# Gate columns in matmuls of 512 tokens, heads transposed before they are split, and the pairs of branch C ahead of those of branch B, in a three-branch encoder layer

## The chip, the cores and the metric

The kernel runs on one core of one Trainium2 chip. Its time is the device time of one execution in microseconds (us); runs are compared by their median. Inside the core, TensorE (PE) multiplies matrices, VectorE (DVE) and ScalarE (ACT) read PE's results out of PSUM and work on them, GpSimd (POOL) does further element-wise work on SBUF, and SyncE (SP) issues every DMA. Each engine takes its instructions strictly in the order that was fixed when the program was built; engines wait for one another by semaphores.

## The reference

One layer over 2048 tokens of width 1024, all in float32. `h` is the LayerNorm of `x`, and one projection of `h` (7592 columns) feeds three branches and all gates:

```
h = layer_norm(x)
proj = h @ w_in        # a_q a_k a_v a_gate  i_q i_k i_w  b_q b_k b_v b_gate  c_q c_gate  m_gate
A: scores = sum_h i_w * relu(i_q . i_k);  the 256 best keys of each query;  8-head attention on these
B: 4 heads, softmax(q0 k0) - lam * softmax(q1 k1), times v, RMS norm
C: 4-head cross attention of c_q into 256 memory tokens (mem @ w_mem_kv)
y_r = (o_r * silu(gate_r)) @ w_proj_r          for r = A, B, C
merged = sum_r sigmoid(m_gate_r) * y_r
out = layer_norm(alpha * h + merged @ w_out)
```

Queries and keys of A, B and of the index scores are rotated (RoPE) on a part of their channels. Keys are limited to the query's own chunk of 64 tokens and all before it.

## The kernel before, in words

**Precision.** Every float32 product is made of three matmuls (`mm3`, L71 to L74): each operand is split into a high part H, rounded to PE's fast float32 format (fp32r), and a rest L = value - H. `split` (L62 to L69) makes the two: a copy into H on one engine, a subtraction into L on another.

**Stages in the order of the text.** The activations are kept transposed, channels on partitions, in four tiles `hP` of 256 tokens each (1024 tokens, a half), and each half is projected in turn.

1. `dense_ai(0)`: queries of A, the index projections, for half 0; `topk_group` finds the 256 best keys of each query for blocks of 128 tokens by a search over the 32 bits of the score (counts on DVE and ACT); `dense_b(0)`, then the same for half 1, two more `topk_group`s, `dense_b(1)`.
2. Attention B: 4 heads x 16 blocks = 64 blocks. Logits (`lg`, L623, L624), row minimum on DVE, exponentials on ACT, a combination on DVE, transposes (`pt`, L703), a split of these by ACT and DVE, and the product with v (`ops`, L709).
3. Attention A: 16 blocks x 4 units of two heads: `lg`, DVE (`AP`, L626), ACT, transposes (`apt`, L777), split (`apr`), product (`aops`, L782).
4. `dense_g(1)`, reload of half 0, `dense_g(0)`: c_q, the SiLU gates (`sg`) and the merge gates (`tm`), 20 jobs of 256 columns for each half (PSUM tile `dps`), with the memory's keys and values between.
5. For each pair of blocks (256 tokens): branch B, then branch C (`attn_c`, cross attention, PSUM tile `cps`), each followed by its output projection (`branch`, PSUM tile `yps`), and a sum on POOL that is stored as `mg_d`.
6. Branch A's projection (`stage1`), then for each pair the output projection (`stage2`, PSUM tile `fz`) and the last LayerNorm.

**What sets the order.** A scheduler places every engine's instructions by a planned timeline. Text order is only a priority: where an attention would leave PE idle, later work whose inputs and buffers are there is put in between. So the gate jobs of step 4 stand between the matmuls of steps 1 and 2, and steps 5 and 6 between those of step 3. Work put between in this way is called filler here.

**What the change touches.** `heads_out` (L212) writes queries and keys transposed to DRAM. Each of its two blocks of 128 tokens is split by DVE first (`dt`: a CAST at L68 and a TENSOR_TENSOR at L69), H and L of a head side by side; PE then transposes the fp32r tile (L223) and ACT copies the result into `de` (L225). RoPE (L133 to L136) runs on POOL ahead of it. `dense` (L244) computes a gate job: for c_q, the merge gates and C's SiLU gate the weights `w` are the stationary operand, for the SiLU gates of A and B the tokens are. Either way a matmul has 256 moving columns. `emit` (L297) evaluates and stores; `gated` (L827) multiplies an attention output by its gate, transposes it and splits it; `yw` is the pool of the tiles `yt` (8 of them, YT) in which merge gates are loaded and branch outputs are made.

Of the kernel before, what the change touches and what calls it, by code (L numbers as in the profile page):

```python
# [23 lines left out]
NP = NB // 2  # L24
KT = D // 128
# [13 lines left out]
YT = 8  # L39
# [14 lines left out]
def tile_layer(ctx, tc, x, mem, ln_in_g, ln_in_b, w_in, w_mem_kv, diff_lambda, diff_norm_g,  # L54
# [28 lines left out]
    qa_d = [[dram(f"qa_d{j}_{p}", [4, 128, 256]) for p in range(NP)] for j in range(2)]  # L83
    qi_d = [[dram(f"qi_d{j}_{p}", [128, 4, 256]) for p in range(NP)] for j in range(2)]
# [5 lines left out]
    qb_d = [[dram(f"qb_d{j}_{p}", [4, 128, 256]) for p in range(NP)] for j in range(2)]  # L90
    kb_d = [[dram(f"kb_d{j}_{p}", [4, 128, 256]) for p in range(NP)] for j in range(2)]
# [3 lines left out]
    cq_d = [dram(f"cq_d{p}", [128, 4, 2, 256]) for p in range(NP)]  # L95
    sg_d = [[dram(f"sg_d{r}_{p}", [128, 4, 256] if r == 2 else [2, 128, 512]) for p in range(NP)] for r in range(3)]
    tm_d = [[dram(f"tm_d{r}_{p}", [128, KT, 256]) for p in range(NP)] for r in range(3)]
    oa_d = [dram(f"oa_d{b}", [128, 512]) for b in range(NB)]
    ob_d = [dram(f"ob_d{b}", [128, 512]) for b in range(NB)]
    mg_d = [dram(f"mg_d{p}", [128, KT, 256]) for p in range(NP)]  # L100

# [45 lines left out]
    hT, hP = {}, {}  # L147
    early = [True]
    last_rope = [None]

    def hT_tile(b):
        if b % 2 == 0:
            hP[b // 2] = hTp.tile([128, 2, KT, 256], F32R, name=f"hP{b // 2}", tag=f"hP{b // 2 % 4}")
        hT[b] = hP[b // 2][:, :, :, 128 * (b % 2):128 * (b % 2 + 1)]
        return hT[b]
# [31 lines left out]
    def prologue(b, banks):  # L187
# [11 lines left out]
        to_hT(hT_tile(b), xt, banks)  # L199

    def save_hT(b):
        xt = p1.tile([128, KT, 128], F32, name="xt")
        G.tensor_tensor(xt, hT[b][:, 0].bitcast(F32), hT[b][:, 1].bitcast(F32), op=ALU.add)
        SP.dma_start(ht_d[b], xt)

    def reload(b):
        xt = p1.tile([128, KT, 128], F32, name="xt")
        SP.dma_start(xt, ht_d[b])
        h = hT_tile(b)
        split(h[:, 0], h[:, 1], xt, A, V)  # L210

    def heads_out(o, nh, d, dup, stores, p):  # L212
        e = dp.tile([128, nh, 2, 128], F32R, name="de")
        for i in range(2):
            t = dp.tile([128, nh, 2 * dup, d], F32R, name="dt" if nh > 1 else "dt1", bufs=3 if nh > 1 else 2)
            src = o[:, i, :, None, :].to_broadcast([128, nh, dup, d]) if dup > 1 else o[:, i, :, None, :]
            split(t[:, :, 0:dup], t[:, :, dup:2 * dup], src, V, V)
            if i:
                pt = dq2.tile([128, nh, 128], F32R, name="psT")
            else:  # L220
                pt = dqs.tile([128, nh, 128], F32R, name="dpt", bufs=1)
# [4 lines left out]
        for dst, c0, c1 in stores:  # L226
            SP.dma_start(dst, e.bitcast(F32)[:, c0:c1].rearrange("p c i t -> p c (i t)"))
# [16 lines left out]
    def dense(kind, half, cols, idx, w=None):  # L244
        n = sum(c for _, c in cols)
        if w is None:
            w = load_win(cols, A if early[0] else G)
        for p in range(4 * half, 4 * half + 4):
            ps = dqs.tile([128, 2, 256], F32, name="dps")
            for i in range(2):  # L250
                if kind in ("cq", "tm") or (kind == "sg" and idx[0] == 2):
                    c = slice(i * 128, (i + 1) * 128)
                    h = hP[p]
                    for k in range(KT):
                        mm3(ps[:, i], w[:, 0, k, c], w[:, 1, k, c], h[:, 0, k], h[:, 1, k], k == 0, k == KT - 1)
                    continue
                h = hT[2 * p + i]
# [5 lines left out]
    def dense_ai01(half):  # L263
# [16 lines left out]
        for p in range(4 * half, 4 * half + 4):  # L280
            ps = [dqs.tile([128, 512], F32, name="dps") for _ in range(2)]
            for a in range(2):
                for i in range(2):
                    h = hT[2 * p + i]
# [11 lines left out]

    def emit(kind, idx, p, ps, n, o=None):  # L297
        if kind == "cq":
            for i in range(2):
                o = dw.tile([128, 2, 256], F32R, name="do", bufs=3)  # L300
                with tc.high_priority():
                    split(o[:, 0], o[:, 1], ps[:, i], A, V)
                SP.dma_start(cq_d[p][:, 2 * idx + i], o.bitcast(F32))
            return
        if kind != "bv" and o is None:
            o = dw.tile([128, 2, 256], F32, name="do", bufs=3)
        if kind in ("sg", "tm"):
            r, j = idx
            with tc.high_priority():
                A.activation(o, ps, AF.Tanh, scale=0.5)  # L310
                if kind == "sg":
                    V.scalar_tensor_tensor(o, o, 1.0, ps, op0=ALU.add, op1=ALU.mult)
            if kind == "tm" or r == 2:
                SP.dma_start((sg_d if kind == "sg" else tm_d)[r][p][:, 2 * j:2 * j + 2], o)
            else:
                SP.dma_start(sg_d[r][p][:, :, j * 256:(j + 1) * 256].rearrange("i p c -> p i c"), o)
            return
        if kind == "bv":
            v = dp.tile([128, 2, 2, 2, 128], F32R, name="de")
# [27 lines left out]
        else:  # L347
# [8 lines left out]
            for i in range(2):  # L356
                PE.transpose(pt[:, i], t[:, i].rearrange("p a d -> p (a d)"), idr)
# [713 lines left out]
```

## Time and profile before

| | |
|---|---|
| median of 3 runs | 2966.72 us (2961.39 to 2970.45) |
| the profiled execution: its span, first to last instruction | 2965.9 us |
| PE busy | 2830.5 us, 95% |
| DVE busy | 2279.2 us, 77% |
| ACT / POOL busy | 1442.6 us, 49% / 983.2 us, 33% |
| DMA engines busy, mean | about 41% |

No time of its own is recorded for the profiled execution beside its span; the span lies 0.8 us under the median of the runs. A busy share counts from an instruction's start to its end. Successive matmuls overlap, so the step from one matmul's start to the next start, not the duration, is what one costs in a stream.

### The profile page before, as it was taken

How to read it: one execution, taken by the hardware profiler on the slowest of the kernel's cores; microseconds unless marked ns; L12 is line 12 of the kernel's file. 1: busy time of each engine (PE TensorE's matmuls, PEld its weight loads, DVE VectorE, ACT ScalarE, POOL GpSimd, SP SyncE). 2: the span in 40 equal slices, each digit the busy share in tenths (PEclk: the TensorE clock that was granted, in tenths of full speed). 3: DMA queues.
4: the chain of work that ended last, by engine and by line, in shares of the span. 5: the costliest groups of instructions: out<-in, count | busy, mean ns of one | idle time of the engine just before them, and what ended most of it. 6: DMA issues, size and time to landing. Idle time of an engine off the chain costs nothing. (4 is left out here: it accounts for less than half of the span.)

```text
span 2965.9 us, 57460 instructions
## 1 busy us (share of the span) xinstructions
PE 2830.5 (95%) x21616; PEld 2715.7 (92%) x21616; DVE 2279.2 (77%) x5309; ACT 1442.6 (49%) x2806; POOL 983.2 (33%) x1064
## 2 busy tenths in 40 slices
PE   7979998999999998999999999999999999988998
PEld 6979998999999998999999999988999999978887
DVE  6499988999899998676667766658787777776655
ACT  4345673677266772333344334446566556544100
POOL 6663547242522236323324222302222222200221
PEclk9999999999999999999999999999999999999999
DMA  6554434433232234624234242273433333256532
GB/s 208 171 191 138 159 113 156 133 119 114 94 101 76 82 93 147 201 73 140 89 118 142 77 128 80 75 242 110 133 114 119 102 113 102 86 172 224 172 131 79
DMA packets 320949, 379.47 MB, mean 128 GB/s; under 512 B 26400, under 2 KB 236832, under 8 KB 320160
## 3 DMA queue, kind: packets, MB, share of 16 engines
q1 hardware_dynamic: 320672, 375.80, 40.2%
q8 instruction: 171, 2.80, 0.4%
q14 instruction: 106, 0.87, 0.1%
HBM read 236.02 MB, written 139.69 MB: 127 GB/s over the span
## 5 line engine op out<-in xcount | busy, mean ns | idle before, releaser
L72 PE MATMUL dps<-hP,w 128*128 128x256 f32 x2048 | 582.6, 284 | 15.1 <-DVE do L69 9.9
L74 PE MATMUL dps<-hP,w 128*128 128x256 f32 x2048 | 581.7, 284 | 0.0
L73 PE MATMUL dps<-hP,w 128*128 128x256 f32 x2048 | 581.2, 284 | 0.0
L72 PE MATMUL dps<-w,hP 128*128 128x256 f32 (+1 forms) x1664 | 491.1, 296 | 12.5 <-POOL w L64 3.1
L73 PE MATMUL dps<-w,hP 128*128 128x256 f32 (+1 forms) x1664 | 490.0, 295 | 0.0
L74 PE MATMUL dps<-w,hP 128*128 128x256 f32 (+1 forms) x1664 | 487.9, 294 | 0.0
L72 PEld LDWEIGHTS dps<-hP,w 128*128 128x128 f32 x2048 | 392.6, 192 | 21.6 <-DVE do L69 10.7
L74 PEld LDWEIGHTS dps<-hP,w 128*128 128x128 f32 x2048 | 392.5, 192 | 4.4 <-POOL w L69 0.3
L73 PEld LDWEIGHTS dps<-hP,w 128*128 128x128 f32 x2048 | 392.7, 192 | 3.6
L533 ACT ACTIVATE ja<-sall,thr 128x1280 bf16<-128x1280 f32 (+4 forms) x224 | 302.2, 1349 | 122.6 <-DVE thr L529 107.1
L64 POOL TENSOR_SCALAR w<-wr 128x1024 fp32r<-128x1024 f32 x120 | 135.5, 1129 | 629.5 <-PE dps L74 404.9
L72 PEld LDWEIGHTS dps<-w,hP 128*128 128x128 f32 x1664 | 324.0, 195 | 16.8 <-issue 4.3
L69 POOL TENSOR_TENSOR w<-wr,w 128x1024 fp32r<-128x1024 f32 (+1 forms) x128 | 332.1, 2595 | 15.0 <-ACT w L66 6.9
L520 DVE TENSOR_SCALAR_CACHE_REDUCE jd<-sall,thr 128x1408 bf16<-128x1408 f32 (+6 forms) x231 | 330.9, 1433 | 5.9
L73 PEld LDWEIGHTS dps<-w,hP 128*128 128x128 f32 x1664 | 324.3, 195 | 1.8
L74 PEld LDWEIGHTS dps<-w,hP 128*128 128x128 f32 x1664 | 323.8, 195 | 2.2
L691 ACT ACTIVATE P<-P,nm 128x128 f32<-128x128 f32 (+15 forms) x128 | 154.1, 1204 | 197.8 <-DVE nm L690 187.5
L626 DVE CUSTOM_DVE_ANT_0 AP<-lg,bias 128x512 f32<-128x512 f32 (+3 forms) x304 | 181.9, 619 | 68.4 <-PE lg L624 25.1
L66 ACT CAST apr<-apt 128x512 fp32r<-128x512 f32 (+1 forms) x288 | 158.4, 563 | 141.7 <-PE apt L777 108.4
L633 DVE TENSOR_SCALAR_CACHE_REDUCE P<-lg 128x512 f32<-128x512 f32 (+3 forms) x288 | 170.4, 596 | 72.3 <-PE lg L624 71.2
L493 DVE SCALAR_TENSOR_TENSOR sall<-ir,iw,sall 128x512 f32<-128x512 f32 (+3 forms) x266 | 217.1, 865 | 8.9 <-ACT ir L489 8.0
L782 PE MATMUL aops<-apr,VA 128*128 128x256 f32 x1088 | 206.7, 297 | 16.8 <-DVE apr L69 6.7
(249 smaller groups left out, 7109.2 us busy)
## 6 DMA issues: line engine op xcount, KB each, us to landing
wr<-in_w_in_dram SPq DMA_DIRECT2D x112, 512.0 KB, 3.9
tm_d<-do SPq DMA_DIRECT2D x96, 256.0 KB, 2.1
bq<-qb_d SPq DMA_DIRECT2D x128, 128.0 KB, 3.1
aq<-qa_d SPq DMA_DIRECT2D x128, 128.0 KB, 3.1
yt<-tm_d SPq DMA_DIRECT2D x64, 256.0 KB, 3.6
sg_d<-do SPq DMA_DIRECT2D x48, 256.0 KB, 2.1
ys<-sg_d SPq DMA_DIRECT2D x48, 256.0 KB, 3.1
facc<-mg_d SPq DMA_DIRECT2D x48, 256.0 KB, 4.1
```

The lines of the kernel that those rows point to most:

```text
L66: A.copy(H, src)
L69: el.tensor_tensor(L, src, H.bitcast(F32), op=ALU.subtract)
L72: PE.matmul(ps, lH, rH, start=start, stop=False)
L73: PE.matmul(ps, lH, rL, start=False, stop=False)
L74: PE.matmul(ps, lL, rH, start=False, stop=stop)
L493: V.scalar_tensor_tensor(s[:, c0:c0 + cn], r[:, :cn], iw[:, h:h + 1], s[:, c0:c0 + cn], op0=ALU.mult, op1=ALU.add)
L520: V.tensor_scalar(jd[:, :L], sc[b], t.bitcast(F32)[:, i:i + 1], None, op0=op, op1=ALU.add, accum_out=dst[:, i:i + 1])
L533: A.activation(ja[:, :L], sc[b], AF.Sign, bias=thr.bitcast(F32)[:, i:i + 1], scale=-1.0, accum_out=cnt[:, i:i + 1])
L626: V.tensor_tensor_reduce(P[:, c0:c0 + cn], ps[:, :cn], bias[:, c0:c0 + cn], scale=-0.125, scalar=-LOW, op0=ALU.add, op1=ALU.min, accum_out ...
L633: V.tensor_scalar(P[:, c0:c0 + n0], ps[:, :n0], -0.125, None, op0=ALU.mult, op1=ALU.min, accum_out=mx[:, col, nch:nch + 1])
L691: A.activation(p[:, :L], p[:, :L], AF.Exp, bias=nm[:, c:c + 1], scale=-1.0, accum_out=sm[:, c:c + 1])
L782: PE.matmul(o_ps.rearrange("p a d -> p (a d)"), VA[:, k0 + i], pr[:, a, i].rearrange("p e q -> p (e q)"), start=(k0 + i == 0 and a == 0), ...
```

## The change

- **Gates by 512 tokens.** The four `hP` tiles become one tile `H4` (two groups of 512 tokens). Every gate job now has the weights stationary and 512 tokens moving: a matmul of 512 columns in place of two of 256. The jobs, their weights and the number of PSUM tiles stay; all gates are stored transposed.
- **Heads in 32 bits.** `heads_out` transposes the float32 projection itself, two groups of up to 128 channels at a time, and splits the transposed result straight out of PSUM (ACT copies H, DVE subtracts). The CAST and the subtraction ahead of the transposes go. Layouts in DRAM and the loads of queries and keys follow; index queries are loaded by four DMAs of 32 partitions where one of 128 was.
- **`gated`**: transposes the ungated output, multiplies on DVE, copies on ACT, subtracts on POOL.
- **All eight pairs of branch C, then all of branch B.** C's results are stored as `mc_d` and loaded again for the sum with B's.
- **YT is 4** in place of 8.

```diff
-YT = 8
+YT = 4
+    H4 = hTp.tile([128, 2, 2, KT, 512], F32R, name="H4")
+    def hT_of(b):
+        return H4[:, b // 4 % 2, :, :, 128 * (b % 4):128 * (b % 4 + 1)]
-    def heads_out(o, nh, d, dup, stores, p):
-        e = dp.tile([128, nh, 2, 128], F32R, name="de")
-        for i in range(2):
-            t = dp.tile([128, nh, 2 * dup, d], F32R, name="dt" if nh > 1 else "dt1", bufs=3 if nh > 1 else 2)
-            src = o[:, i, :, None, :].to_broadcast([128, nh, dup, d]) if dup > 1 else o[:, i, :, None, :]
-            split(t[:, :, 0:dup], t[:, :, dup:2 * dup], src, V, V)
-            if i:
-                pt = dq2.tile([128, nh, 128], F32R, name="psT")
-            else:
-                pt = dqs.tile([128, nh, 128], F32R, name="dpt", bufs=1)
-            for c in range(nh):
-                PE.transpose(pt[:, c], t[:, c].rearrange("p a d -> p (a d)"), idr)
-            with tc.high_priority():
-                A.copy(e[:, :, i], pt)
+    def heads_out(o, groups, stores):
+        n = len(groups)
+        e = dp.tile([128, 2, n, 2, 128], F32R, name="de", bufs=4)
+        turn[0] ^= 1
+        if turn[0]:
+            pt = dq2.tile([128, n, 2, 128], F32, name="psT")
+        else:
+            pt = dqs.tile([128, n, 2, 128], F32, name="dpt", bufs=1)
+        for u, (c0, cn) in enumerate(groups):
+            for i in range(2):
+                PE.transpose(pt[:cn, u, i], o[:, i, c0:c0 + cn], idf)
+        for u0, u1 in ((0, 2),) if groups[-1][1] == 128 else ((0, n - 1), (n - 1, n)):
+            cn = groups[u0][1]
             with tc.high_priority():
+                split(e[:cn, 0, u0:u1], e[:cn, 1, u0:u1], pt[:cn, u0:u1], A, V)
 ...
     def dense(kind, half, cols, idx, w=None):
+        if kind in ("cq", "sg", "tm"):
+            for q in range(2 * half, 2 * half + 2):
+                for g in range(2):
+                    c = slice(g * 128, (g + 1) * 128)
+                    ps = dqs.tile([128, 512], F32, name="dps")
+                    for k in range(KT):
+                        mm3(ps, w[:, 0, k, c], w[:, 1, k, c], H4[:, q % 2, 0, k], H4[:, q % 2, 1, k], k == 0, k == KT - 1)
+                    with tc.high_priority():
+                        emit_gate(kind, idx, g, q, ps)
+            return
 ...
+    def emit_gate(kind, idx, g, q, ps):
 ...
+        r, j = idx
+        o = dw.tile([128, 512], F32, name="do", bufs=3)
+        A.activation(o, ps, AF.Tanh, scale=0.5)
+        if kind == "sg":
+            V.scalar_tensor_tensor(o, o, 1.0, ps, op0=ALU.add, op1=ALU.mult)
+        SP.dma_start((sg_d if kind == "sg" else tm_d)[r][q][:, 2 * j + g], o)
 ...
-                SP.dma_start(qi.bitcast(F32), qi_d[j][b // 2][:, :, (b % 2) * 128:(b % 2 + 1) * 128])
+                for r in range(4):
+                    SP.dma_start(qi.bitcast(F32)[32 * r:32 * r + 32], src[r // 2])
 ...
-        eng.tensor_tensor(o, o, s, op=ALU.mult)
 ...
-            A.activation(oT[:, 0, :, t], ps, AF.Copy, scale=0.5)
-            V.scalar_tensor_tensor(oT[:, 1, :, t], ps, 0.5, oT[:, 0, :, t].bitcast(F32), op0=ALU.mult, op1=ALU.subtract)
+            V.scalar_tensor_tensor(s, ps, 0.5, s, op0=ALU.mult, op1=ALU.mult)
+            A.copy(oT[:, 0, :, t], s)
+            G.tensor_tensor(oT[:, 1, :, t], s, oT[:, 0, :, t].bitcast(F32), op=ALU.subtract)
 ...
-    for p in range(NP):
-        T = []
-        for r, w, mix in ((1, wb, gated_b), (2, wc, gated_c)):
+    for r, w, mix in ((2, wc, gated_c), (1, wb, gated_b)):
+        for p in range(NP):
 ...
                 branch(yq, w, oT, u, t, 1)
-        for u in range(4):
-            G.tensor_tensor(T[u], T[u], T[4 + u], op=ALU.add)
-            SP.dma_start(mg_d[p][:, 2 * u:2 * u + 2], T[u])
+                if r == 2:
+                    SP.dma_start(mc_d[p][:, 2 * u:2 * u + 2], t)
+                    continue
+                c = yw.tile([128, 2, 256], F32, name="yt")
+                SP.dma_start(c, mc_d[p][:, 2 * u:2 * u + 2])
+                G.tensor_tensor(t, t, c, op=ALU.add)
+                SP.dma_start(mg_d[p][:, 2 * u:2 * u + 2], t)
```

Where the change stands in the programs is shown by the order of the engines' rows (line, operation, tiles as out<-in, shape, how many in a run). First PE in the first half of attention B (`lg`, `ops` and `pt` are the attention's, `dps` is gate filler). Before:

```order
L709 MATMUL ops<-vg,pr 128x256 x7
L703 MATMUL pt<-idf,P 128x128 x5
L623 MATMUL lg<-kg,bq 128x512
L624 MATMUL lg<-kg,bq 128x512
L623 MATMUL lg<-kg,bq 128x512
L624 MATMUL lg<-kg,bq 128x512
L74 MATMUL dps<-hP_25611,w 128x256
```

and now, at the same place:

```order
L715 MATMUL ops<-vg,pr 128x256 x15
L709 MATMUL pt<-idf,P 128x128 x6
L629 MATMUL lg<-kg,bq 128x512
L630 MATMUL lg<-kg,bq 128x512
L629 MATMUL lg<-kg,bq 128x512
L630 MATMUL lg<-kg,bq 128x512
L75 MATMUL dps<-H_269,w 128x512
```

In the gap behind the second pair of logits, up to the next `lg`, 22 gate matmuls of 256 columns stand before and 20 of 512 now: about as many instructions, and nearly twice the columns.

Second, PE in the last third of attention B (`yps` is branch C's projection, `cps` its cross attention). Before:

```order
L709 MATMUL ops<-vg,pr 128x256 x7
L703 MATMUL pt<-idf,P 128x128 x6
L623 MATMUL lg<-kg,bq 128x512
L624 MATMUL lg<-kg,bq 128x512
L623 MATMUL lg<-kg,bq 128x512
L624 MATMUL lg<-kg,bq 128x512
L73 MATMUL dps<-hP_25620,w 128x256
```

and now:

```order
L74 MATMUL cps<-mkT,cqT 128x256
L715 MATMUL ops<-vg,pr 128x256 x15
L709 MATMUL pt<-idf,P 128x128 x8
L629 MATMUL lg<-kg,bq 128x384
L630 MATMUL lg<-kg,bq 128x384
L629 MATMUL lg<-kg,bq 128x512
L630 MATMUL lg<-kg,bq 128x512
L73 MATMUL yps<-yoT,H_269 128x256
```

The gates are over by then: branch C's work is the filler, which before began only with attention A.

Third, PE at the end of attention A, ahead of the first `fz` (`gT` is a transpose of branch A's output). Before:

```order
L72 MATMUL yps<-yoT,whP_33902 128x256
L73 MATMUL yps<-yoT,whP_33902 128x256
L74 MATMUL yps<-yoT,whP_33902 128x256
L833 MATMUL gT<-idf,fo 128x128 x8
L72 MATMUL fz<-whP_34237,fmT 128x512
```

and now:

```order
L788 MATMUL aops<-apr,VA_14503 128x256 x3
L783 MATMUL apt<-idf,AP 128x128 x4
L788 MATMUL aops<-apr,VA_14503 128x256 x8
L794 MATMUL ot<-idf,os 128x128 x4
L73 MATMUL fz<-H_269,fmT 128x512
```

Nothing stands any more between the last instruction of attention A and the first output projection.

## Rows read from the trace of the kernel before

**Rows 1.** The page: span; busy time of each engine (share of the span).
```profile
span 2965.9 us, 57460 instructions
PE 2830.5 (95%) x21616; PEld 2715.7 (92%) x21616; DVE 2279.2 (77%) x5309; ACT 1442.6 (49%) x2806; POOL 983.2 (33%) x1064
```
**Rows 2.** Busy time by stretch: from:to, length, each engine's busy time, clock, DMA.
```profile
0.00:1200.60 1200.60, 1112.45 (x8886) 1097.35 (x8887) 1051.03 (x1804) 674.17 (x1183) 554.38 (x533) 0.97 0.41 133
1200.60:1637.00 436.40, 433.10 (x3381) 419.13 (x3380) 310.41 (x1060) 172.59 (x341) 146.20 (x208) 1.00 0.39 119
1637.00:1963.50 326.50, 325.10 (x2551) 316.04 (x2550) 202.87 (x668) 125.85 (x226) 87.12 (x132) 1.00 0.33 103
1963.50:2739.80 776.30, 741.47 (x5685) 698.55 (x5683) 586.04 (x1593) 449.18 (x1025) 145.74 (x144) 0.99 0.45 134
2739.80:2966.00 226.20, 218.40 (x1120) 184.61 (x1120) 128.89 (x188) 20.86 (x35) 49.76 (x47) 0.98 0.38 132
```
**Rows 3.** Timeline of PE, gate matmuls of 256 columns: start, duration.
```profile
749.73 0.28 PE L74 MATMUL dps<-hP,w 128*128 128x256 f32 x1
...
755.97 0.28 PE L72 MATMUL dps<-hP,w 128*128 128x256 f32 x1
```
**Rows 4.** Timeline of PE, output projection, matmuls of 512 columns.
```profile
2849.68 0.39 PE L72 MATMUL fz<-whP,fmT 128*128 128x512 f32 x1
...
2855.98 0.39 PE L72 MATMUL fz<-whP,fmT 128*128 128x512 f32 x1
```
**Rows 5.** Timeline of PE: transposes of fp32r tiles, then of a float32 tile.
```profile
648.79 0.46 PE L223 MATMUL dpt<-idr,dt 128*128 128x128 f32 x4
649.09 0.51 PE L223 MATMUL psT<-idr,dt 128*128 128x128 f32 x4
649.44 0.35 PE L74 MATMUL dps<-hP,w 128*128 128x256 f32 x1
...
2301.80 0.60 PE L777 MATMUL apt<-idf,AP 128*128 128x128 f32 x4
2302.15 0.37 PE L73 MATMUL yps<-yoT,whP 128*128 128x256 f32 x1
```
**Rows 6.** Line 223, PE's idle time before it (us, times).
```profile
  DVE dt L69: 38.4, 28
```
**Rows 7.** Groups of DVE instructions: busy us, mean ns, idle before.
```profile
L69 DVE TENSOR_TENSOR dt<-do,dt 128x256 fp32r<-128x256 f32 x128 | 76.1, 620 | 0.2
L68 DVE CAST dt<-do 128x256 fp32r<-128x256 f32 x128 | 50.0, 415 | 42.8 <-POOL do L136 31.9 <-PE dpt L223 8.7 <-PE psT L223 1.4
```
**Rows 8.** The same for branch C's cross attention, in attention A's stretch.
```profile
L870 DVE TENSOR_REDUCE cmx<-cps 128x2 f32<-128x512 f32 x32 | 22.0, 686 | 2.3 <-PE cps L74 2.3
L69 DVE TENSOR_TENSOR cpr<-cps,cpr 128x512 fp32r<-128x512 f32 x32 | 21.9, 684 | 1.4 <-ACT cpr L66 1.1
L899 DVE TENSOR_TENSOR yoT<-co,yoT 128x256 fp32r<-128x256 f32 x32 | 14.4, 451 | 0.6 <-ACT yoT L898 0.4
L896 DVE TENSOR_TENSOR co<-co,cps 128x256 f32<-128x256 f32 x32 | 13.2, 414 | 0.8 <-ACT co L895 0.4
```
**Rows 9.** Timeline of DVE in attention A.
```profile
2302.94 0.69 DVE L626 CUSTOM_DVE_ANT_0 AP<-lg,bias 128x512 f32<-128x512 f32 x1
2303.55 0.68 DVE L845 SCALAR_TENSOR_TENSOR yt<-yt,yps 128x512 f32<-128x512 f32 x1
```
**Rows 10.** Busy time of the first third of attention A.
```profile
1963.50:2218.00 254.50, 241.11 (x1829) 224.97 (x1828) 203.89 (x632) 163.93 (x410) 51.77 (x52) 0.99 0.50 145
```
**Rows 11.** The chain that ended last, from attention A to `fz`.
```profile
2732.79 6.21 DMA facc<-mg_d
2739.78 0.80 PE fz L72
```
**Rows 12.** POOL's sum of `yt`; loads of `yt` (KB, us to landing).
```profile
L922 POOL TENSOR_TENSOR yt<-yt 128x512 f32<-128x512 f32 x32 | 43.1, 1347 | 117.3 <-DVE yt L845 103.1 <-DVE crc L877 14.2
yt<-tm_d SPq DMA_DIRECT2D x64, 256.0 KB, 3.6
```

More of the change, by code (lines that the diff above doesn't have):

```diff
@@ L24 @@
 NP = NB // 2
+NQ = NB // 4
 KT = D // 128
@@ L82, in tile_layer @@
     h_d = [dram(f"h_d{b}", [128, D]) for b in range(NB)]
-    qa_d = [[dram(f"qa_d{j}_{p}", [4, 128, 256]) for p in range(NP)] for j in range(2)]
-    qi_d = [[dram(f"qi_d{j}_{p}", [128, 4, 256]) for p in range(NP)] for j in range(2)]
+    qa_d = [[dram(f"qa_d{j}_{p}", [2, 256, 256]) for p in range(NP)] for j in range(2)]
+    qi_d = [[dram(f"qi_d{j}_{p}", [2, 128, 256]) for p in range(NP)] for j in range(2)]
     ka_d = dram("ka_d", [128, S])
@@ L89, in tile_layer @@
     bias_d = [dram(f"bias_d{b}", [128, (b + 1) * 128], BF16) for b in range(NB)]
-    qb_d = [[dram(f"qb_d{j}_{p}", [4, 128, 256]) for p in range(NP)] for j in range(2)]
-    kb_d = [[dram(f"kb_d{j}_{p}", [4, 128, 256]) for p in range(NP)] for j in range(2)]
+    qb_d = [[dram(f"qb_d{j}_{p}", [2, 256, 256]) for p in range(NP)] for j in range(2)]
+    kb_d = [[dram(f"kb_d{j}_{q}", [2, 256, 512]) for q in range(NQ)] for j in range(2)]
     vb_d = [[dram(f"vb_d{j}_{p}", [2, 128, 2, 256]) for p in range(NP)] for j in range(2)]
@@ L250, in dense @@
             for i in range(2):
[L251 to L257, printed above, removed]
+                h = hT_of(2 * p + i)
                 for k in range(KT):
@@ L283, in dense_ai01 @@
                 for i in range(2):
-                    h = hT[2 * p + i]
+                    h = hT_of(2 * p + i)
                     for k in range(4):
@@ L295, in dense_ai01 @@
                 emit("ai1", None, p, None, W_AI - 256, o[1])
-    def emit(kind, idx, p, ps, n, o=None):
-        if kind == "cq":
-            for i in range(2):
-                o = dw.tile([128, 2, 256], F32R, name="do", bufs=3)
-                with tc.high_priority():
-                    split(o[:, 0], o[:, 1], ps[:, i], A, V)
-                SP.dma_start(cq_d[p][:, 2 * idx + i], o.bitcast(F32))
-            return
+    def emit_gate(kind, idx, g, q, ps):
+        if kind == "cq":
+            for a in range(2):
+                o = dw.tile([128, 512], F32R, name="do", bufs=3)
+                if a == 0:
+                    A.copy(o, ps)
+                    H = o
+                else:
+                    V.tensor_tensor(o, ps, H.bitcast(F32), op=ALU.subtract)
+                SP.dma_start(cq_d[q][:, 2 * idx + g, a], o.bitcast(F32))
+            return
+        r, j = idx
[4 more added lines that the diff above has]
+        SP.dma_start((sg_d if kind == "sg" else tm_d)[r][q][:, 2 * j + g], o)
+    def emit(kind, idx, p, ps, n, o=None):
         if kind != "bv" and o is None:
             o = dw.tile([128, 2, 256], F32, name="do", bufs=3)
[L307 to L317, printed above, removed]
         if kind == "bv":
-            v = dp.tile([128, 2, 2, 2, 128], F32R, name="de")
+            v = dp.tile([128, 2, 2, 2, 128], F32R, name="de", bufs=4)
             with tc.high_priority():
@@ L904, in gated_b @@
             SP.dma_start(o, ob_d[b])
-            gated(yp, yq, "cps", o, yp.tile([128, 512], F32, name="ys"), 1, b, G, oT)
+            gated(yp, yq, "cps", o, yp.tile([128, 4, 128], F32, name="ys"), 1, b, oT)
     def gated_c(p, oT):
```

99 lines of the change are left out of this document (47 added, 52 removed).

## The prediction

> **What bounds the kernel now.** I read the page first, then the busy time by stretch, then the timeline of PE for the step between matmuls, and last who waited for whom. The page shows PE busy for 95% of the 2965.9 us span and DVE for 77% [rows 1]. That share counts overlapping durations, so I took the step between starts instead: 52 gate matmuls of 256 columns from 749.73 to 755.97 are 0.120 us each [rows 3], 27 of 512 columns from 2849.68 to 2855.98 are 0.233 [rows 4]. I cut the span where the work changes: before the first transpose of attention B (1200.6 us), B's first 40 blocks (436.4), its last 24 (326.5), attention A up to the first output projection (776.3), and the rest (226.2) [rows 2]. The reader should see that PE is busy 93 to 100% of every stretch while DVE comes close only in the first (1051 of 1201) and falls to 203 of 326.5 and 129 of 226 behind it. So PE's queue sets the time, and two things matter: how much PE has to do, and in which order, because a stretch with too little filler waits for DVE instead. The granted clock is 0.97 to 1.00 of its upper level, 2.4 GHz, in all five [rows 2], so little is to be had there.
>
> The span lies 0.8 us under the median of the runs, so I make the sum against 2965.9 and read it as the median.
>
> **The change part by part.**
>
> *Gates.* 20 jobs, two halves, 192 matmuls of 256 columns each half-job: 7680 x 0.120 = 921.6 us. Now 3840 x 0.2333 = 896.0. That is 25.6 us less, if a gate matmul of 512 columns runs at the step of the output projection, which has the same shape and the same kind of operands. The bounds are 25.6 less and nothing (a step of two old ones, 0.240): the same columns pass, so I see no cause for a loss. The number of PSUM tiles to empty stays (each now 24 matmuls, 5.6 us, before 48, 5.8 us), so ACT, DVE and POOL get no more to do per gate. The projection rows show 0.233 at 512 columns. The Trainium skill, in "TensorE: Matmul & The Clock Gate", section "Back-to-back issue gap", gives about 131 ns as the sustained step at 512 columns, and about 216 for an isolated one. By 131 the gates alone would fall by some 419 us; the trace does not agree, neither with that nor with 216 (it has 233), and the measured step decides.
>
> *Heads.* 544 transposes of fp32r tiles become 256 of float32 tiles. Eight of the old take 0.65 us from 648.79 to 649.44, 0.081 each; four float32 ones take 0.35, 0.0875 each [rows 5]. 544 x 0.081 - 256 x 0.0875 = 44.2 - 22.4 = 21.8 us less on PE. On DVE a CAST (0.415) and a subtraction (0.620) [rows 7] per 128 tokens leave the path in front of the transposes; one subtraction out of PSUM per 256 tokens comes in behind them. PE stood idle 38.4 us in 28 waits for exactly that DVE work [rows 6]. What is late next is RoPE on POOL, for which DVE itself waited 31.9 us [rows 7]; PE now waits for it directly. Each wait gets shorter by the two DVE steps, 1.035 us: 28 x 1.035 = 29 us, between 0 (POOL late anyway) and 38.4. I take 29.
>
> *Order.* This is the part that costs. The gaps of the attention were filled by the planner with about as many gate matmuls as before, 22 of 256 columns against 20 of 512 in the gap shown. Counted over the whole program, the stretches become:
>
> - Before B: 7262 matmuls of 256 columns, now 3072 of 256 and 2286 of 512: 901.9 against 871.4 us, 30.5 more; transposes 21.8 less, 16 memory transposes moved here, 1.4 more; waits 29 less. 1200.6 + 10.1 - 29 = 1182.
> - B's first 40 blocks: 2059 of 256 (247.1 us) become 1524 of 512 and 192 of 256 (378.6), minus the memory's 1.4 us: 130 more. PE was busy 433 of 436 there [rows 2], so all of it lies on the path: 566.
> - B's last 24 blocks: 1581 gate matmuls (189.7 us) go, 30 of 512 stay (7.0). Branch C comes in: 136 matmuls of `cps` (16.3), 52 narrow ones (3), 56 transposes (4.9), 288 of `yps` (34.6). PE has 123 us less to do: 204. Now DVE is late: 202.9 us were its own [rows 2]; C's four groups are 71.5 us for 320 `cps` matmuls [rows 8], 136 of them 30.4; 13 more weight splits and 12 `yt` at 0.69 [rows 9] are 17. That is 250 us. Lower end: successive instructions start 0.61 apart and not 0.69 [rows 9], 250 x 0.88 = 220. Upper end: in the first third of A DVE reached 204 of 254.5, 80% [rows 10], 250 / 0.80 = 312. I take 262, near the middle. Queued behind a late DVE are the splits of `pt`, and behind them PE's `ops`.
> - A to the first `fz`: 330 matmuls of 256 (39.6), 136 `cps` (16.3), 52 narrow ones (3), 44 transposes (3.9) and 2 logits (0.5) have moved forward, 63 us. 5 of them were cover: before, 40 `yps` stood beside the wait from 2732.79 to 2739.78 for the load of `mg_d` [rows 11]; now nothing does. 776.3 - 63 + 5 = 718.
> - The rest: 12 transposes less, 225.
>
> Sum: 1182 + 566 + 262 + 718 + 225 = 2953 us, 13 less than 2965.9. In one line: 47 us of PE work and 29 of waits are saved, 58 are given back where PE waits for DVE, 5 at the seam.
>
> *What I cost at nothing.* `gated`: the product moves from POOL or DVE ahead of the transposes to DVE behind them, and a subtraction from DVE to POOL. 32 of each, on engines that PE does not wait for; without that cover 32 x 0.7 us. C's results take a way through DRAM: 64 transfers more, and 92 more for other layouts. YT 4: a step of B holds two tiles for a load of 3.6 us [rows 12], 24 matmuls (2.9), DVE (0.7), POOL's sum (1.35) [rows 12] and a store of about the load's length, 12 us, two steps at a time, so one step every 6 us. The 32 steps stand in a stretch of some 300 us, 9 us apart. That cover gone, SP would hold back loads of A queued behind a `yt`.
>
> **The rivals.**
>
> *PE stays full.* If DVE's load in the last third of B hides behind PE, the stretch takes its PE work, 204, and the seam its old length: 2953 - 58 - 5 = 2890. For it: DVE's rows overlap, and ACT shares the splits. Against it: even at 0.61 a step DVE needs 220.
>
> *The tail of B starves, slower.* The place is the same, B's last 24 blocks, and the price is the upper end: 312 instead of 262 gives 3003. For it: where PE had too little filler before, at the start of A, both engines together left a fifth of DVE's time unused [rows 10]. Against it: there the chain through ACT was that of A, with 4 tiles `AP` for 1024-wide exponentials; B's blocks overlap better (PE lost 1.4 us of 326.5 [rows 2]). It turns to slower than before from 275 us in that stretch.
>
> *Nothing saved by the width.* If a gate step of 512 is 0.240 or the planner's gaps swallow the waits of the heads again, 26 or 29 us return: 2980.
>
> *The step of the skill's page.* With 0.131 the time would be near 2535.
>
> **How the numbers follow.** The forecast's own case, 2930 to 2975, has 0.50; PE full 0.19; the starved tail 0.21; nothing saved 0.09; the page's step 0.01. About 0.3% (9 us) is what a measurement of this kernel tells from no change: faster is below 2958, slower above 2976. Of the forecast's own case 0.31 lies below 2958 and 0.17 between. Faster: 0.31 + 0.19 + 0.01 and a little of the others, 0.52. Same: 0.18. Slower: 0.30. The range takes in PE full at the low end, 2890, and the starved tail with part of the heads' 29 us lost, 3018.
>
> **What would show it.** Gate matmuls of 512 columns 0.233 apart; no wait for a `dt`, and waits of the heads' transposes for POOL's L136 in their place, under 15 us. First transpose of B at about 1182, its 41st block at 1748, A's first transpose at 2010, `fz` at 2728. In B's last 24 blocks DVE over 90% busy and PE under 85%. The forecast is wrong if PE is busy over 95% there (then the time is under 2920), if the stretch before B still takes 1200 us, or if SP's waits on `yt` show up in front of A's loads.

## The result and the profile after

The changed kernel takes 3031.8 us (median of 4 runs, 3031.3 to 3032.7), the kernel before 2967.0 beside it: ratio 1.0217, 95% interval 1.0202 to 1.0232. It is slower by 65 us; the forecast was 2953 and its range ended at 3018.

The page of the changed kernel, answering to [rows 1]: busy time of each engine, with its share of the span.

```profile
span 3029.5 us, 49112 instructions
PE 2823.2 (93%) x17488; PEld 2509.3 (83%) x17488; DVE 2196.4 (72%) x5053; ACT 1400.0 (46%) x2718; POOL 1014.4 (33%) x1080
```

Every engine but POOL is less busy than before, and the span is 64 us longer. So work was saved, and more than that went into waits. Its busy time by stretch, cut at the same five places as [rows 2]:

```profile
0.00:1216.50 1216.50, 1117.36 (x6712) 1006.32 (x6712) 999.04 (x1573) 638.01 (x1105) 570.25 (x539) 0.97 0.41 132
1216.50:1780.80 564.30, 558.74 (x3020) 480.43 (x3019) 312.99 (x1057) 188.32 (x365) 191.40 (x238) 1.00 0.38 114
1780.80:2050.70 269.90, 232.80 (x1536) 201.99 (x1534) 228.04 (x782) 141.18 (x298) 72.36 (x137) 0.96 0.42 124
2050.70:2805.00 754.30, 697.33 (x5120) 637.29 (x5119) 531.04 (x1463) 412.79 (x918) 127.92 (x117) 0.98 0.45 138
2805.00:3029.50 224.50, 216.92 (x1108) 183.33 (x1108) 125.24 (x181) 19.68 (x33) 52.45 (x49) 0.98 0.37 127
```

| stretch | before | forecast | measured | miss |
|---|---|---|---|---|
| before B | 1200.6 | 1182 | 1216.5 | +34.5 |
| B, first 40 blocks | 436.4 | 566 | 564.3 | -1.7 |
| B, last 24 blocks | 326.5 | 262 | 269.9 | +7.9 |
| A to the first `fz` | 776.3 | 718 | 754.3 | +36.3 |
| the rest | 226.1 | 225 | 224.5 | -0.5 |

The three stretches in the middle and at the end came out as worked out, with PE at 86% in B's last 24 blocks (233 of 270; 100% before) and DVE at 84%, a little short of the 90% that I had named. Two failed: the one in front of B, over the 1200 us that the forecast named as a sign of being wrong, and A's. Three views follow.

First, the gates' step. Of a run of gate matmuls in the timeline of PE (start, duration), the first and the last of 13:

```profile
699.69 0.39 PE L74 MATMUL dps<-H,w 128*128 128x512 f32 x1
...
702.41 0.39 PE L74 MATMUL dps<-H,w 128*128 128x512 f32 x1
```

2.72 us for 12 steps: 0.227, better than the 0.233 taken from [rows 4]. 3840 of them are 870 us, 51 under the 921.6 that the forecast counted for the old ones, and 44 under them at the step of 0.119 used in the counts below. The width does save PE's time.

Second, the heads. What PE waited for at line 223's transposes (us in total, times, longest), before and now:

```profile
PE psT L223 <- DVE dt L69: 13.3, 8, 6.1
PE dpt L223 <- DVE dt L69: 12.3, 8, 3.8
```
```profile
PE psT L223 <- POOL do L138: 10.6, 6, 4.2
PE dpt L223 <- POOL do L138: 0.2, 1, 0.2
```

The 38.4 us in 28 waits of [rows 6] are not PE's alone: the row adds the idle time of the weight loads (PEld), which have a row of their own and run beside the matmuls. On PE it was 25.6 us in 16 waits. The waits for `dt` are gone, and 10.8 us of waits for RoPE on POOL have come in their place: 14.8 saved where 29 were credited.

Third, the indexer ahead of B. It scores block after block for top-k: `ips` on PE, relu to `ir` on ACT, a weighted sum to `sall` on DVE. Its blocks 13 and 14 begin at 835.1, 862.2 and end at 889.0 in the kernel before, 27 us each; in the changed one at 807.7, 850.7 and 892.9, 43 and 42. Groups by line of that stretch, 808 to 893 us, of the changed kernel (busy us, mean ns, idle before); a third of the gate matmuls is in the row of each of lines 73 to 75:

```profile
L73 PE MATMUL dps<-H,w 128*128 128x512 f32 x104 | 40.6, 391 | 0.0
L490 PE MATMUL ips<-KI,qi 128*128 128x256 f32 x122 | 17.9, 277 | 0.0
L499 DVE SCALAR_TENSOR_TENSOR sall<-ir,iw,sall 128x512 f32<-128x512 f32 (+2 forms) x56 | 48.1, 920 | 29.7 <-ACT ir L495 29.7
```

The same stretch, 793 to 846.5 us, of e4 (heads alone, gates of 256; below):

```profile
L73 PE MATMUL dps<-H,w 128*128 128x256 f32 x110 | 31.2, 284 | 0.0
L505 PE MATMUL ips<-KI,qi 128*128 128x256 f32 x120 | 22.6, 277 | 0.0
L514 DVE SCALAR_TENSOR_TENSOR sall<-ir,iw,sall 128x512 f32<-128x512 f32 (+3 forms) x56 | 43.5, 831 | 3.6 <-ACT ir L510 3.2
```

Between about 120 `ips` in both stand 312 gate matmuls where there were 330: nearly as many, each nearly twice as long. DVE, which is busy 90 of the 96 us from 750 to 846 in e4, now stands idle 29.7 us for scores, and the search behind it starts later. The last scan of top-k on DVE, of before, e4, the changed kernel and e12 (the width alone):

```profile
1171.97 4.42 DVE L568 TENSOR_TENSOR_SCAN pf<-ones,ja 128x2048 f16<-128x2048 bf16 x1
```
```profile
1122.94 5.26 DVE L589 TENSOR_TENSOR_SCAN pf<-ones,ja 128x2048 f16<-128x2048 bf16 x1
```
```profile
1186.80 5.71 DVE L574 TENSOR_TENSOR_SCAN pf<-ones,ja 128x2048 f16<-128x2048 bf16 x1
```
```profile
1237.22 6.61 DVE L573 TENSOR_TENSOR_SCAN pf<-ones,ja 128x2048 f16<-128x2048 bf16 x1 [2.83 <-POOL ja L570]
```

The heads alone bring the last scan of top-k forward by 49 us; with the width behind them it comes 55 later again (e2, 1177.83), in the whole change 64.

What of PE's work counts in front of B shows when the stretch is cut at the last `ips`, behind which no score waits for PE any more. The row of the last run of them, before, e4, e2 (heads and width) and changed:

```profile
915.08 0.40 PE L484 MATMUL ips<-KI,qi 128*128 128x256 f32 x2
873.25 0.40 PE L505 MATMUL ips<-KI,qi 128*128 128x256 f32 x2
921.73 0.64 PE L490 MATMUL ips<-KI,qi 128*128 128x256 f32 x4
930.73 0.64 PE L490 MATMUL ips<-KI,qi 128*128 128x256 f32 x4
```

| kernel | last `ips` starts | PE work up to it | difference | from there to B | PE work in that |
|---|---|---|---|---|---|
| before | 915 | 796 | 119 | 285 | 262 |
| e4 | 873 | 746 | 127 | 288 | 263 |
| e2 | 922 | 801 | 121 | 286 | 256 |
| changed | 931 | 801 | 130 | 285 | 256 |
| e12 | 975 | 845 | 130 | 292 | 260 |
| e10 | 927 | 801 | 126 | 263 | 172 |
| e11 | 875 | 746 | 129 | 282 | 248 |

PE work is counted as in the next section. Up to the last score the time is PE's work and 119 to 131 us of waits, in all sixteen kernels that were measured. Behind it 282 to 292 us pass in fifteen of them, and 263 in e10. With the width PE has 55 us more to do in front of the last score (e4 to e2): 1168 gates of 512 columns, 265 us, stand there in place of 1765 of 256, 210 us. Behind the last score B waits for top-k: SP issues the store of the last mask (`pf`) and after it the first load of `kg`, with which B begins. Before, changed, e10:

```profile
1183.78 0.32 SPq L572 DMA_DIRECT2D bias_d<-pf  x1
1188.86 0.59 SPq L651 DMA_DIRECT2D kg<-kb_d  x1
```
```profile
1197.86 0.32 SPq L578 DMA_DIRECT2D bias_d<-pf  x1
1201.50 0.61 SPq L657 DMA_DIRECT2D kg<-kb_d  x1
```
```profile
1162.85 14.69 SPq L589 DMA_DIRECT2D bias_d<-pf  x2
1180.23 0.60 SPq L670 DMA_DIRECT2D kg<-kb_d  x1
```

### The profile page after: what moved, and what is told of

The parts are those of the page before. It is cut to its first block, busy times and chain, and to the rows that moved or that the text cites. A ratio compares the mean times of both kernels' runs of the same rounds, so it can differ in the third digit from the quotient of the medians.

```text
span 3029.5 us, 49112 instructions
## 1 busy us (share of the span) xinstructions
PE 2823.2 (93%) x17488; PEld 2509.3 (83%) x17488; DVE 2196.4 (72%) x5053; ACT 1400.0 (46%) x2718; POOL 1014.4 (33%) x1080
## 5 line engine op out<-in xcount | busy, mean ns | idle before, releaser
L73 PE MATMUL dps<-H,w 128*128 128x512 f32 x1280 | 507.0, 396 | 22.5 <-DVE do L319 12.8
L74 PE MATMUL dps<-H,w 128*128 128x512 f32 x1280 | 505.0, 395 | 1.3 <-DVE H L70 1.3
L75 PE MATMUL dps<-H,w 128*128 128x512 f32 x1280 | 504.9, 394 | 0.5 <-POOL w L70 0.5
L73 PE MATMUL dps<-w,H 128*128 128x256 f32 (+1 forms) x1152 | 343.7, 299 | 16.2 <-POOL w L65 8.4
L74 PE MATMUL dps<-w,H 128*128 128x256 f32 (+1 forms) x1152 | 343.6, 298 | 5.7 <-POOL w L70 5.7
L75 PE MATMUL dps<-w,H 128*128 128x256 f32 (+1 forms) x1152 | 342.0, 298 | 0.0
L73 PEld LDWEIGHTS dps<-H,w 128*128 128x128 f32 x1280 | 243.0, 190 | 75.9 <-DVE do L319 10.6
L74 PEld LDWEIGHTS dps<-H,w 128*128 128x128 f32 x1280 | 243.1, 190 | 50.6 <-DVE H L70 2.0
L75 PEld LDWEIGHTS dps<-H,w 128*128 128x128 f32 x1280 | 243.0, 190 | 50.0 <-POOL w L70 0.8
L499 DVE SCALAR_TENSOR_TENSOR sall<-ir,iw,sall 128x512 f32<-128x512 f32 (+3 forms) x266 | 234.3, 936 | 52.7 <-ACT ir L495 51.3
L73 PEld LDWEIGHTS dps<-w,H 128*128 128x128 f32 x1152 | 225.9, 196 | 19.1 <-POOL w L65 9.1
L788 PE MATMUL aops<-apr,VA 128*128 128x256 f32 x1088 | 213.7, 303 | 23.4 <-DVE apr L70 10.2
L74 PEld LDWEIGHTS dps<-w,H 128*128 128x128 f32 x1152 | 225.9, 196 | 7.2 <-POOL w L70 6.6
L73 PE MATMUL yps<-yoT,H 128*128 128x256 f32 x768 | 221.9, 290 | 8.3 <-DVE yt L849 5.3
L75 PEld LDWEIGHTS dps<-w,H 128*128 128x128 f32 x1152 | 225.8, 196 | 0.8
L70 DVE TENSOR_TENSOR apr<-apt,apr 128x512 fp32r<-128x512 f32 (+1 forms) x288 | 185.4, 656 | 53.8 <-ACT apr L67 50.9
```

The source lines that it names most:

```text
L70: el.tensor_tensor(L, src, H.bitcast(F32), op=ALU.subtract)
L73: PE.matmul(ps, lH, rH, start=start, stop=False)
L74: PE.matmul(ps, lH, rL, start=False, stop=False)
L75: PE.matmul(ps, lL, rH, start=False, stop=stop)
L499: V.scalar_tensor_tensor(s[:, c0:c0 + cn], r[:, :cn], iw[:, h:h + 1], s[:, c0:c0 + cn], op0=ALU.mult, op1=ALU.add)
L788: PE.matmul(o_ps.rearrange("p a d -> p (a d)"), VA[:, k0 + i], pr[:, a, i].rearrange("p e q -> p (e q)"), start=(k0 + i == 0 and a == 0), ...
```

## The experiments

"PE work" is a count: the instructions that PE's order has in a stretch, by the steps measured (0.2265 for every matmul of 512 columns, 0.119 for 256, 0.0875 for a float32 transpose, others in proportion). Output projections and logits step at 0.233, which leaves some 11 us of the whole program out. Whole program: before 2674, changed 2609. B runs from its first transpose to A's first.

### The three parts, alone and together

| kernel | heads | width | C first, YT 4 | us | ratio (95%) | B starts | A starts | first `fz` |
|---|---|---|---|---|---|---|---|---|
| before | | | | 2967 | 1 | 1200.6 | 1963.5 | 2739.8 |
| e4 | x | | | 2964.4 | 0.998 (0.997 to 1.000) | 1160.9 | 1933.6 | 2738.3 |
| e12 | | x | | 3033.4 | 1.021 (1.017 to 1.026) | 1266.7 | 2026.6 | 2809.2 |
| e2 | x | x | | 3005.1 | 1.012 (1.010 to 1.015) | 1207.6 | 1994.0 | 2775.7 |
| e3 | x | | x | 3033.7 | 1.022 (1.020 to 1.024) | 1156.8 | 1925.1 | 2770.2 |
| changed | x | x | x | 3031.8 | 1.022 (1.020 to 1.023) | 1216.5 | 2050.7 | 2805.0 |

All but the kernel before have the new `gated` and the weights stationary in every gate job; no run has these alone.

**e2**, the changed kernel with the pair order of before:

```diff
-    for r, w, mix in ((2, wc, gated_c), (1, wb, gated_b)):
-        for p in range(NP):
+    for p in range(NP):
+        for r, w, mix in ((1, wb, gated_b), (2, wc, gated_c)):
...
-YT = 4
+YT = 8
```


> The changed kernel with one part undone: in each pair branch B's projection and then C's, added in SBUF, 8 tiles yt, no way through DRAM. Theory S: C no longer comes into B's tail, which has even less filler (136 us of PE work in the last 24 blocks instead of 195) but DVE also has about 45 us less there, so about 230 instead of 270; A gets that work back, 666 us of PE work instead of 608, about 775 instead of 754; total 2995 to 3025, so within 1% of the changed kernel. Theory Y: A's waits go, A to the first output projection 720 or less, total under 2975.

3005, as S expected; B's last 24 blocks 221 (S: 230), A 782 (S: 775). Branch C in B's tail had cost its own length: 49 us more for 58 more of PE work. Y's figure for A was missed by far.

**e3**, the changed kernel with gates of 256 (dense gets the pair loop of before; C first stays):

```diff
-            for q in range(2 * half, 2 * half + 2):
+            for p in range(4 * half, 4 * half + 4):
...
-                        mm3(ps, w[:, 0, k, c], w[:, 1, k, c], H4[:, q % 2, 0, k], H4[:, q % 2, 1, k], k == 0, k == KT - 1)
+                        mm3(ps[:, g], w[:, 0, k, c], w[:, 1, k, c], H4[:, p // 2 % 2, 0, k, tk], H4[:, p // 2 % 2, 1, k, tk], k == 0, k == KT - 1)
```


> The changed kernel with one part undone: gates of 256 tokens, the new heads and the new pair order stay. Theory S: gates fill B to its end as in the kernel before, first transpose of B near 1170, A's first at 1935, total 2940 to 2960 (2653 us of PE work by steps and the 290 of waits of before). Theory Y: A still waits, total 2985 or more. Theory H: first transpose of B stays at 1200 or later.

Theory S fell here, and Y's total holds: with B full to its end (A starts at 1925) the order C first and the four tiles still cost 69 us against e4. A takes 845 where e4 has 805, and the part behind the first `fz` 262 where e4 has 226, with 528 projection matmuls instead of 312. A has 64 units, four to a block of queries. Busy time of e3 from its 61st unit to the first `fz`, then what SP's queue waited for from 2580 to 2820:

```profile
2531.50:2770.20 238.70, 182.53 (x1341) 173.14 (x1340) 94.92 (x173) 54.75 (x96) 62.70 (x49) 0.89 0.63 200
```
```profile
SPq L944 <- DMA mg_d<-yt: 52.3, 22, 5.5
SPq L965 <- DMA mg_d<-facc: 17.8, 9, 2.8
SPq L946 <- POOL yt L945: 17.2, 19, 2.3
```

With C alone in front, one chain of C comes with 96 projection matmuls to fill A with, and not 192 of B and C. So the planner's order has 216 of them from A's 49th to its 56th unit where e4's has 361, and 1104 from there to the first `fz` where e4's has 576. There branch B's projection stands alone, a step about 8 us long: a store (2.6 to 4.1), a load from `mc_d` (2.2 to 3.7), POOL's sum (1.3), one behind the other. No engine is busy 80% in that stretch.

**e4**, the heads alone (e3's gates and e2's order):

> The kernel before with the heads part alone: gates of 256 tokens, old pair order, 8 tiles yt; heads transposed in 32 bits. Theory S: the 21 us of PE work that the heads save arrive, and of the 29 of waits for dt about half come back as waits for POOL: total 2935 to 2955. Theory H (POOL in front of the heads' transposes, and ACT and DVE behind them, give it all back): 2960 or more, first transpose of B at 1200 or later.

2964: H's total, but not for H's reason, for B starts at 1160.9, 40 us early, with 48 us of PE work less in front of it (21.8 heads, 26 gates that the planner left for later). What was gained went again in B (10 us) and A (28), most of it at the start of A, where 250 gates now run and 42 did before (A's first 12 units 112 us, before 89.5).

**e12**, the width alone (old heads, old order):

> The kernel before with the width alone: gates of 512 tokens; heads in fp32r as before, pair order of before, 8 tiles yt. By the two mechanisms found so far (gate matmuls are placed by number, so the indexer of blocks 13 and 14 takes 43 us each instead of 27, and B's last 24 blocks run out of gates): first transpose of B 30 to 50 later than before (1230 to 1250), B near 785, A to the first output projection near 780 with 30 us of gates gone from it, total 3015 to 3045, so slower than before by as much as the width costs behind the new heads (e2 against e4: 41). If the width costs only together with the heads, total 2945 to 2980.

3033, as the first expectation has it, though B starts 17 us later than its range (1266.7) and takes 760 us and not 785, for 652 us of PE work.

### Does holding the gates back give the time back?

**e1**, whole tiles of half 0 held behind blocks of B, C first:

```diff
+        n = tiles[0]
+        tiles[0] += 1
+        if n < HOLD:
+            return nullcontext()
+        return tc.issue_after(first[lgs[(n - HOLD) * len(lgs) // (80 - HOLD)]])
...
-                    for k in range(KT):
+                    with nullcontext() if half else held():
+                        for k in range(KT):
```


> The changed kernel whole, but 65 of the 80 gate tiles of half 0 may not start before a given block of attention B, spread over all 64 blocks by their length. Theory S (the loss is starvation: B's first 40 blocks use up the gates, so its last 24 and A wait for DVE): B from its first transpose to A's first falls from 834 to about 705 (683 us of PE work by steps), C's units move back into A, A to the first output projection stays near 745, the last part grows from 224 to 250 with the projection work moved there, total 2900 to 2930. Theory Y (four tiles yt and the way of C's results through DRAM hold loads up in A): B may fall, but A keeps its waits and the work pushed into it costs what B gains, total 2980 or more. Theory H (heads on POOL cost before B): nothing changes there in any case, first transpose of B at 1216.

3029.1 (ratio 1.020), S missed by 100 and Y's total met. B shrank from 834 to 800 only, A kept 757, and the part behind the first `fz`, with 504 projection matmuls instead of 288, grew from 224 to 261: what B gained was lost there.

**e5**, the same with the pair order of before; **e6**, nothing held, half 0 by 256 and half 1 by 512; **e9**, e5 in pieces of 3 matmuls, each behind its own step of B:

> Both of e1 and e2 at once: 65 gate tiles of half 0 held back over the blocks of attention B, and the pair order of before with 8 tiles yt. Gates of 512 and the new heads stay. Theory S (two separate losses: B's tail starves because the gates of 512 are used up, and the order C first bunches branch B's projection behind A): both are gone, B from 1210 to about 1975, A to the first output projection 780, total 2940 to 2970, in any case 35 us or more under e2. Theory E (attention B can't be covered with 352 us of gates in coarse pieces, however they are spread: what is held back only moves the waits): B stays at 785 or more, total 2990 to 3010, as e2.

> New heads, pair order of before, 8 tiles yt; gates of half 1 by 512 (most of what stands before B), gates of half 0 by 256 (what stands beside B), nothing held back. Theory S: the number of gate matmuls decides how far the filler reaches; B's first 56 blocks take what they take in the kernel before (about 690), the last 8 have 150 matmuls left instead of 434 and lose at most 15; first transpose of B near 1208, A's first near 1915, total 2930 to 2950, under heads alone (2964). Theory E: with 22 us less PE work in all the waits rise by as much, total 2960 or more.

> As e5 (gates of 512, new heads, pair order of before, 65 tiles of half 0 held back), but held back in pieces of 3 matmuls, each behind its own step of attention B (a chunk of logits or a group of `ops`), instead of in whole tiles of 24. In e5, B took 791 us for 662 us of PE work. Theory G (the pieces are too coarse there: 24 matmuls run at once and later steps have nothing): B 700 to 735, total 2935 to 2965. Theory E (352 us of gates can't cover B however they are spread): B 770 or more, total 2990 or more.

3011.8 (1.015), 2989.9 (1.007) and 3013.3 (1.016): theory E's numbers, e5 2 us over its total; G's piece size made no difference. B takes 786.4 in e2 and 791.3 and 786.0 in e5 and e9, all with 678 us of PE work in it, spread or not (e9's expectation says 662; the count is 678). Busy time of B in e9:

```profile
1218.10:2004.10 786.00, 727.56 (x4021) 619.38 (x4020) 503.08 (x1717) 293.00 (x555) 226.52 (x334) 0.97 0.36 106
```

In e6 it takes 766.6 for 701, in e4 772.7 for 738, in the kernel before 762.9 for 737, in e12 759.9 for 652. Less PE work in B hardly makes it shorter. Part of the reason is at A's start. What PE waited for longest there, in e9:

```profile
PE lg L642 <- DMA aq<-qa_d: 18.9, 1, 18.9
```

In the program A's tiles take the place in SBUF that B's leave, and in e9 these loads are issued from 1987.0 on, right behind B's last store. In the kernel before, gates ran to the end of B and 42 matmuls beyond, and no such wait is among PE's there; in e2, e5, e6, e9 and e12 no gate is left for it, and PE waits 13 to 19 us.

**e10**, e9 with all 80 tiles kept for B; **e11**, e10 with half 1 by 256:

> As e9, with all 80 tiles of half 0 kept for attention B (15 of them, 83 us, ran before B in the changed kernel, where PE was full already). Theory G with P (before B a gate costs its full time): first transpose of B 1135 to 1150, B 775 to 800 for 761 us of PE work, total 2915 to 2945. Theory E: B 830 or more, total 2985 or more.

> As e10, with the gates of half 1 (before B) by 256 as in the kernel before. Theory I (the same number of gate matmuls stands between the indexer's, by 512 twice as long, so the scores of blocks 13 to 15 reach DVE 16 us late each): the indexer's blocks 13 and 14 take 27 us each again instead of 43, first transpose of B 15 or more earlier than in e10 though PE has 22 us more to do, total under e10. Against it (PE is full there and only its work counts): first transpose of B 15 to 25 later than in e10.

3052.6 (1.029) and 3025.4 (1.019). e10 went as theory E has it, with 849 us for B. The 15 tiles that the changed kernel runs before B (83 us) are gone from there, and B starts only 27 us earlier. PE waits instead, for the load of `kg`. Its wait, and that of SP's queue from 1000 to 1230 us for the last masks of top-k (`pf`):

```profile
PE lg L642 <- DMA kg<-kb_d: 82.9, 1, 82.9
```
```profile
SPq L589 <- DVE pf L588: 59.2, 4, 19.8
```

So behind the last score it is not PE that sets the end, but top-k's chain on DVE and ACT. e11 has 22 us more PE work in front of B and starts B 31.8 us earlier, at 1157.7, its indexer at 27 us a block again. That is theory I, both of its numbers, and its total, under e10. It also settles the rival that PE is simply full there: by that, 22 us more work would have come out as a later start; they are 55 less ahead of the last score and 77 more behind it. The 47 us by which B starts later in e2 than in e4 look like that rival, since PE work in front of B also rose by 47; the table above shows which part of it counts, the 55 us more ahead of the last score.

**e13**, half 1 by 256, half 0 by 512: 8 tiles free, 64 in pieces over B, 8 behind B's last block; **e14** with 4 there:

```diff
+        return tc.issue_after(steps[min(n * nsteps // (8 * (80 - FREE - LAST)), nsteps - 1)])
```


> New heads, pair order of before, 8 tiles yt, gates of half 1 by 256, gates of half 0 by 512: 8 of their 80 tiles free (they run before B, where the wait for top-k's end stands), 64 spread over attention B in pieces of 3 matmuls, the last 8 held back behind B's last block, where e5, e6 and e9 waited 14 to 19 us for the load of aq. Theory P (the width costs by placement alone): first transpose of B near 1160 as with heads alone, B 740 to 760 with the seam covered, A 805 as with heads alone, total 2930 to 2955, under heads alone (2964). Theory W (the longer matmuls cost by themselves: an instruction of attention that becomes ready waits 0.23 us for the one in front and not 0.12, and the order of a held piece fits worse): B 773 or more, total 2965 to 2990 in spite of 22 us less PE work.

> As e13 with 4 tiles behind B's last block instead of 8, and 68 in B. Theory P: B's own part gets 20 us more PE work and the seam 22 us less cover: 5 to 25 over e13, with a wait for aq of 5 to 15 us again. Theory W: within 5 us of e13.

2974.0 (1.0025, 1.0014 to 1.0036) and 2974.5: 31 us under e2, 39 under e9, 10 over e4. In e13 B starts at 1163.6, and the wait for `aq` is 2 us; e14 has none, with half the cover, and is within 5 us of e13, as W expected. Taking the width out of the indexer and covering the seams returns 31 of the 41 us that it cost together with the heads; theory P's total is missed by 19 and W's met. The 22 us of PE work that it saves here still don't show: B takes 799 for 725 of work in e13 and 811 for 743 in e14. That the longer matmuls do this in the way W says was not shown.

### Four tiles or eight

**e7**, the changed kernel with `YT = 8`; **e8**, e3 with it:

> The changed kernel with 8 tiles yt instead of 4, nothing else. Theory Y (the four tiles hold loads and stores up: each step of branch B's projection waits for a store to give a tile back): A to the first output projection falls from 754 to 720 or less, total 3000 or less. Theory O (it is the order itself: with C alone there is half as much projection work for each chain of C, so A has less filler and B's projection bunches at the end): total 3020 to 3040.

> As e3 (gates of 256, new heads, C first) with 8 tiles yt instead of 4. In e3 the steps of branch B's projection stood uncovered from 2600 to 2800, PE waited 82 us there, a step 8 us. Theory Y: with twice the tiles the waits there fall under 45, total 2995 or less. Theory O: the planner leaves the same projections for the end, and the loads, sums and stores of a step take their time one after another: 3020 or more.

3018.2 and 3014.3: 14 and 19 us under their partners with 4 tiles, between the theories. Four tiles cost that; the rest of the order's price stays, 50 us of the 69 with gates of 256 (e8 against e4) and 13 of the 27 with the width (e7 against e2). In e8, too, SP waits for the stores of `mg_d`, 43 us in 21.

## Why the prediction was wrong

**"So PE's queue sets the time."** The step that failed first. It holds up to the last score and not behind it. PE was 93% busy in front of B [rows 2] because the planner fills what DVE and ACT leave; behind the last score that filler stands beside top-k's search, and from there to B it is 282 to 292 us whether PE has 248 or 266 to do; in e10 84 us less of it are worth 23. In front of the last score a gate delays the search by its length. The sum took PE work of the whole stretch at its full length, on both sides of that point. By count that work was even 11 us less than the sum had it (1058 us before and 1056 now, where 10 more were forecast), but the part ahead of the last score rose from 796 to 801 and the waits there from 119 to 130, so B started 16 us later and not 19 earlier. Without the width 746 us stand there (e4): the 49 saved by the heads and by gates left for later were used up by 55 of longer gates. I had seen that the number of gates in a gap stays while their length doubles, and priced it in attention B alone.

**"1200.6 + 10.1 - 29 = 1182."** The 29 us for `dt` were half there (14.8, above). The 28 waits behind the figure were those of PE and of its weight loads together; the rule of 1.035 us a wait gives 17 for the 16 waits of PE, near what was saved, and the waits for POOL in their place, 10.8, stayed under the 15 named. Other waits grew: `ips` on ACT was waited for 15.1 us where it was 9.8, and POOL's `w` 14.1 where it was 4.3.

**B, 566 and 262.** Right in mechanism: gates run out by block 40, and PE waits behind it, for DVE most. The size of the second is near by a choice between 220 and 312: DVE had 228 us to do and not 250, and it filled 84% of the stretch and not over 90. The longest waits of PE in the last 24 blocks:

```profile
PE pt L709 <- DVE P L703: 8.1, 10, 1.5
PE lg L629 <- DVE P L639: 6.4, 5, 3.6
PE cps L890 <- POOL cP L886: 4.6, 4, 1.9
```

What I made of it afterwards, that an even spread would return the loss, was wrong (e5, e9).

**"776.3 - 63 + 5 = 718."** Work did leave A, but I let its waits stay as they were, about 106 us (776 less 670 of PE work), and they rose to 147 (754 less 607). In e2, with the order and the tiles of before, they are 117 (782 less 665), in e7, C first with eight tiles, 126 (772 less 646): most of the rise came with the four tiles and the order. Together these two cost 27 us with the width in place (changed against e2: B takes 48 longer and starts 9 later, A takes 27 less) and 69 without it (e3 against e4). With the width 288 of the 768 matmuls of C's projection already stand in B's starved tail; that the order is cheaper there for that reason was not tested. The seam I priced at 5 us; the chain at the end of A shows the load of `mg_d` uncovered, as expected, and PE idle for 9.4 us at the first `fz`, where it was 2.3:

```profile
2794.91 0.67 PE ot L794 x4
2795.60 0.70 DVE ao L798
2796.78 2.12 DMA oa_d<-ao
2799.34 4.86 DMA facc<-mg_d
2804.29 0.64 ACT fmT L992
2804.97 0.80 PE fz L73
```

**"What I cost at nothing."** YT 4 costs 14 us (e7), 19 with gates of 256 (e8). The way through DRAM costs where no attention stands beside it: I worked out a step every 6 us, two at a time, and in e3 one takes 8; the stretch of 300 us that was to hide the steps was there only for a part of them.

**The rivals.** "Nothing saved by the width" was priced at 26 us; its true price, alone (e12), is some 65. The last of them, 2535, takes 419 us off a total that had 25.6 of them off already; by its own figures it is 2560, which changes no chance. None of my cases had a saving turn into a loss ahead of B, so the range ended too low.

**What stays open.** Why B, in the old order, takes 760 to 811 us for anything from 652 to 743 us of PE work (849 and 854 in e10 and e11, for 761). Its DVE is busy 503 of 786 in e9, so DVE's throughput does not set it; the load at A's start explains 13 to 19 us in five of the runs. In e13 and e14 the pieces were placed by me and not by the planner, and whether a better placing would show the rest was not tried. The best of the measured kernels is e4, the heads alone, 0.2% under before, which is within what this kernel's runs tell from no change.

## What to carry to other kernels

A 95% busy engine that a planner fills with background work is not thereby the bound: find the chain that the filler stands beside, and ask which engine waits for the matmuls between the filler. Filler ahead of such a matmul costs its full length, filler behind the last of them may cost almost nothing. If a planner keeps nearly the number of filler instructions in a gap, making each twice as long delays what shares their queue, and uses the filler up before the stage ends. Time the parts of a change apart: here one of three was harmless, and the prices of the other two (41 and 69) overlap by some 43 us.

## What the runs showed of the hardware

A gate matmul of 512 columns steps at 0.227 us and not at the 0.233 of the output projection with the same shape. Where PE waits a lot the granted clock falls: mean 0.89 in e3 from A's 61st unit to the first `fz`, where PE was busy 183 of 239 us, and 0.85 in e10 from 893 to 1216 us, where PE was busy 230 of 323, against 1.00 in B's first 40 blocks; 1.00 is 2.4 GHz, and a mean under it holds time at the other level, 1.2.
